# Hyena filter spectra: decay and bias rows spread over the partitions by DMA, and the two filters' last products on the two halves of the array's rows

## The chip, the cores and the metric

The kernel runs on one core of a Trainium2 chip. The time is the device time of one execution in microseconds (us). Three runs of the kernel before gave 2129.68 to 2137.14 us, with a median of 2131.46 us. The engines are named as in the profile: PE multiplies matrices (PEld loads its stationary operand), DVE, ACT and POOL work on tiles, SP issues most of the DMAs.

## The reference

The program is two layers of a hybrid trunk over 256 latent and 256 context tokens of width 1024, in fp32. Each layer modulates the tokens (adaLN), projects them, runs attention, RWKV-7 time mixing and a Hyena long convolution side by side, projects back, and ends with a feed-forward block (dense in layer 0, eight experts in layer 1). The change lies in one small piece, which depends on parameters alone and not on the tokens, the spectra of the Hyena filters:

```
h = sin(hy_freq1 * (z @ hy_w1 + hy_b1))          # z: 256 positions x 33
h = sin(hy_freq2 * (h @ hy_w2 + hy_b2))          # 256 x 64
h = (h @ hy_w3) * exp(-t * hy_decay)             # 256 x 1024: 2 filters x (fwd, bwd) x 256
kern = concatenate([fwd, 0, bwd reversed])       # per filter
kern = kern / sum(abs(kern))
K = rfft(kern)                                   # taken with cosine and sine matrices
y = irfft(rfft(z) * K) + z * hy_bias             # later, in the convolution
```

## The kernel before, in words

An fp32 matmul is one call in the code and two passes in the trace, so a row "x4" of such a matmul is two calls. The weights' products are split into high and low parts and take three matmuls (`mm3`, lines 321 to 323).

A scheduler orders the instructions of each engine ahead of time, from the order in which the program issues them and from priorities; at run time each engine takes its own list strictly in that order and waits by semaphores. Buffers come from rings and pools. Loads on SP are issued behind one another (`behind`).

The program begins with a stage called stage 0 below. It loads 16 pieces of 512 KB of the adaLN weights of layer 0 (`raw`, line 347, "wraw<-in_adaw"). Each piece, once landed, feeds four matmuls of 128 rows by 32 columns ("ada", line 392), and their sums are transposed (`adaT`, line 404) and modulate the context's normalised rows, which start the first projection ("u", line 321). The buffers for the pieces come free when PE has used them. Between the ada matmuls PE works on the first layer's spectra (`spectra`, lines 534 to 612). The second layer's spectra are worked out between the RWKV part of layer 1's context and the end of layer 0's latent feed-forward block, whose last product is "fo".

`spectra` computes, in this order: the first product (p1, line 542, "hf"); the exponential windows exp(-t * decay), for which the decay row lies on one partition and is spread over 128 by two matmuls with a row of ones (line 548, "hf_d"), so that ACT reads the spread row from PSUM in four instructions of 128x512 (line 550); two sines, each reduced on DVE and then taken on ACT (`sin_of`, lines 498 to 513), with the second product between them (line 557); the bias row, spread in the same manner (line 563) and copied by ACT (line 564). Then, in two halves of the positions (tt) and for two filters (od), come the last products with a contraction of 64 (line 575, "hf3"), which DVE multiplies by the windows (line 576). ACT takes absolute values (line 580), POOL adds forward and backward parts (line 581), PE sums them over the positions ("hf_n", line 582), and cosine and sine products follow ("Kc", "Ks", "Kn").

Of the kernel before, what the change touches and what calls it, by code (L numbers as in the profile page):

```python
# [143 lines left out]
def layout(i):  # L144

    g = lambda n: np.asarray(i[n])
    A = {}
    A["cst"] = constants()
    xs = np.stack([g("ctx")[0], g("x")[0]])
    A["xs"] = np.ascontiguousarray(xs.reshape(2, 2, 128, D).transpose(0, 2, 1, 3))  # L150
    cc = np.zeros((128, 8, 32), np.float32)
    cc[:, :, 0] = g("c_ctx").reshape(8, 128).T
    cc[:, :, 1] = g("c")[0].reshape(8, 128).T
    A["cc"] = cc
    aw = g("ada_w").reshape(2, 8, 128, 3, 4, 2, 256)
    A["adaw"] = np.ascontiguousarray(aw.transpose(0, 3, 5, 1, 2, 4, 6))
    ab = np.zeros((2, 3, 128, 512), np.float32)
    b = g("ada_b").reshape(2, 3, 4, 512)
    for j in range(4):
        for s in range(2):  # L160
            ab[:, :, 32 * j + s] = b[:, :, j]
    A["adab"] = ab
    ft = feature_tiles()
    wi = g("w_in")
    wp = np.zeros((2, 1024, 20 * 128), np.float32)
    for n, cols in enumerate(ft):
        m = [q for q, c in enumerate(cols) if c >= 0]
        wp[:, :, [n * 128 + q for q in m]] = wi[:, :, [cols[q] for q in m]]
    A["win"] = np.ascontiguousarray(wp.reshape(2, 8, 128, 20, 128).transpose(0, 3, 2, 1, 4))
    wo = g("w_out")[:, mix_rows()]  # L170
    A["wout"] = np.ascontiguousarray(wo.reshape(2, 4, 2, 128, 2, 512).transpose(0, 4, 1, 3, 2, 5))

    def w13(w1, w3):
        e = w1.shape[0]
        u = np.stack([w1, w3], 1).reshape(e, 2, 4, 2, 128, 11, 256)
        return np.ascontiguousarray(u.transpose(0, 5, 2, 4, 3, 1, 6)).reshape(e, 11, 4, 128, 2, 512)

    def w2(w):
        e = w.shape[0]
        u = w.reshape(e, 11, 2, 128, 2, 512)  # L180
        return np.ascontiguousarray(u.transpose(0, 4, 1, 3, 2, 5))

    A["fw13"] = w13(g("ffn_w1"), g("ffn_w3"))[0]
    A["fw2"] = w2(g("ffn_w2"))[0]
    A["mw13"] = w13(g("moe_w1")[0], g("moe_w3")[0])
    A["mw2"] = w2(g("moe_w2")[0])
    A["rout"] = np.ascontiguousarray(g("moe_router")[0].reshape(8, 128, 8).transpose(1, 0, 2))
    A["rows"] = np.stack([g("ln1_g"), g("ln1_b"), g("ln2_g"), g("ln2_b")], 1)
    pr = np.zeros((2, 128, NPRM), np.float32)

    def pp(name, a, col=0, r0=0):
        pr[:, r0:r0 + a.shape[1], PRM[name] + col] = a

    mu = g("rwkv_mu")
    for m, nm in ((0, "mu0"), (1, "mu1")):
        pp(nm, mu[:, m, 768:864], 0)
        for q, o in enumerate((256, 384, 512, 640)):
            pp(nm, mu[:, m, o:o + 128], 1 + q)
        for q, o in enumerate((0, 128)):
            pp(nm, mu[:, m, o:o + 128], 5 + q)  # L200
    sw, sb = g("hy_short_w"), g("hy_short_b")
    for q, o in enumerate((512, 640, 0, 128, 256, 384)):
        for m in range(3):
            pp(f"hw{m}", sw[:, m, o:o + 128], q)
        pp("hb", sb[:, o:o + 128], q)
    for h in range(2):
        pp("qg", g("q_gain"), 0, 64 * h)
        pp("kg", g("k_gain"), 0, 64 * h)
    for d in range(2):
        for t in range(2):  # L210
            pp("a0", g("rwkv_a0")[:, d, 128 * t:128 * t + 128], 2 * d + t)
    for nm, src in (("kk", g("rwkv_kk")), ("ka", g("rwkv_ka")), ("rk", g("rwkv_rk").reshape(2, 256)),
                    ("gng", g("rwkv_gn_g")), ("gnb", g("rwkv_gn_b"))):
        for t in range(2):
            pp(nm, src[:, 128 * t:128 * t + 128], t)
    pp("b1", g("hy_b1"))
    pp("f1", g("hy_freq1"))
    pp("b2", g("hy_b2"))
    pp("f2", g("hy_freq2"))
    A["prm"] = pr  # L220
    lo = np.zeros((2, 128, 2, 512), np.float32)
    wB, aB, gB = g("rwkv_wB"), g("rwkv_aB"), g("rwkv_gB")
    for d in range(2):
        lo[:, 16 * d:16 * d + 16, 0, 256 * d:256 * d + 256] = wB[:, d]
        lo[:, 32, 0, 256 * d:256 * d + 256] = g("rwkv_w0")[:, d]
        lo[:, 32 + 16 * d:48 + 16 * d, 1, 256 * d:256 * d + 256] = aB[:, d]
    lo[:, 64:96, 1, 0:256] = gB
    A["lora"] = lo
    w12 = np.zeros((2, 64, 128), np.float32)
    w12[:, :33, :64] = g("hy_w1")  # L230
    w12[:, :, 64:] = g("hy_w2")
    A["hy12"] = w12
    A["hy3"] = np.ascontiguousarray(g("hy_w3"))
    A["hydec"] = np.ascontiguousarray(g("hy_decay"))
    A["hyd"] = np.ascontiguousarray(g("hy_bias")).reshape(2, 512)
    return A
# [8 lines left out]
AF = mybir.ActivationFunctionType  # L245
# [250 lines left out]
class Mix(Trunk):  # L496

    def sin_of(s, ps, f, fb, out):

        v = s.nc.vector  # L500
        a = s.k([64, 256], "sn")
        n = s.k([64, 256], "sn")
        v.tensor_scalar(a, ps, f, fb, op0=OP.mult, op1=OP.add)
        M = 12582912.0
        v.tensor_scalar(n, a, 1.0 / (2 * math.pi), M, op0=OP.mult, op1=OP.add)
        v.tensor_scalar(n, n, M, None, op0=OP.subtract)
        hi = float(np.float32(6.28125))
        mid = float(np.float32(2 * math.pi - 6.28125))
        lo = float(2 * math.pi - 6.28125 - mid)
        for cst in (hi, mid, lo):  # L510
            v.scalar_tensor_tensor(a, n, -cst, a, op0=OP.mult, op1=OP.add)
        v.tensor_scalar(a, a, 3.1415925, -3.1415925, op0=OP.min, op1=OP.max)
        s.nc.scalar.activation(out, a, AF.Sin)

    def spec_load(s, l):

        def ld(*a):
            with s.behind():
                s.last = s.nc.sync.dma_start(*a)

        w12 = s.k([64, 256], "sn")
        ld(w12[:, :128], s.A["hy12"][l])
        dr, br = s.k([1, 1024], "hydec"), s.k([1, 512], "hyd")
        ld(dr, s.A["hydec"][l:l + 1])
        ld(br, s.A["hyd"][l:l + 1])

        def rest():
            w3 = s.k([64, 1024], "hy3")
            ld(w3, s.A["hy3"][l])
            return w12, w3, dr, br  # L530

        return rest

    def spectra(s, l, bk, b2, bn, w12, w3, dr, br):

        nc = s.nc
        mm = nc.tensor.matmul
        fb = s.k([128, 2], "hy_fb")
        for i in range(2):
            nc.vector.tensor_mul(fb[:64, i:i + 1], s.pv(l, f"f{i + 1}")[:64], s.pv(l, f"b{i + 1}")[:64])  # L540
        p1 = s.bank(bk, "hf1")[:64, :256]
        mm(p1, w12[:33, :64], s.c("zT")[:33, :], start=True, stop=True)

        wins = [s.k([128, 1024], "hy_w") for _ in range(2)]
        for od in range(2):
            ds = slice(512 * od, 512 * od + 512)
            b = s.bank((b2, bn)[od], "hf_d")
            mm(b, s.c("ones")[0:1, :], dr[:, ds], start=True, stop=True)
            for tt in range(2):
                i = nc.scalar.activation(wins[tt][:, ds], b, AF.Exp, scale=s.c("negt")[:, tt:tt + 1])  # L550
                if s.first is not None:
                    s.order(i, s.first)
                    s.first = None
        h1 = s.k([64, 256], "sn")
        s.sin_of(p1, s.pv(l, "f1")[:64], fb[:64, 0:1], h1)
        p2 = s.bank(bk, "hf2")[:64, :256]
        mm(p2, w12[:64, 64:128], h1, start=True, stop=True)
        h2 = s.k([64, 256], "sn")
        s.sin_of(p2, s.pv(l, "f2")[:64], fb[:64, 1:2], h2)
        rb = s.k([128, 2, 512], "hy_rb")  # L560
        rn, dbc = rb[:, 0], rb[:, 1]
        b = s.bank(b2, "hf_d")
        mm(b, s.c("ones")[0:1, :], br, start=True, stop=True)
        nc.scalar.copy(dbc, b)
        yield

        eo = [s.k([128, 2, 2, 256], "hy_eo") for _ in range(2)]
# [2 lines left out]
        for tt in range(2):  # L570
            hf = s.k([128, 2, 2, 256], "hy_f")
            win = wins[tt]
            for od in range(2):
                p3 = s.bank((bk, b2)[od], "hf3")
                mm(p3, h2[:, 128 * tt:128 * tt + 128], w3[:, 512 * od:512 * od + 512], start=True, stop=True)
                nc.vector.tensor_mul(hf[:, od].rearrange("p d c -> p (d c)"), p3, win[:, 512 * od:512 * od + 512])
                if tt == 0:
                    nc.vector.memset(hf[0:1, od, 1, :], 0.0)
            ab = s.k([128, 2, 2, 256], "hy_ab")
# [10 lines left out]
        for kt in range(2):  # L590
# [7 lines left out]
            p2 = s.bank(b2, "Ks")  # L598
# [1157 lines left out]
```

## Time and profile before

| | |
|---|---|
| median of three runs | 2131.46 us |
| the profiled execution | 2134.47 us |
| its span, first to last instruction | 2132.7 us |
| PE busy | 2033.8 us, 95% of the span |
| DVE, ACT, POOL busy | 1659.7, 1105.6, 111.1 us |
| mean granted TensorE clock | 0.965 of full speed |

The profile is one execution. Its time exceeds its span by 1.8 us and the median by 3.0 us. A granted clock of 1.00 stands for 2.4 GHz and 0.50 for 1.2 GHz. Before the first change of clock the column reads 1.00, whatever the level; there the durations of the matmuls tell it. Matmuls are pipelined, so that a row's duration overlaps the next row by some tenths of a microsecond; the differences of start times give the price.

### The profile page before, as it was taken

What the parts mean: (1) busy time and instruction counts of PE and PEld (TensorE: products, weight loads), DVE (VectorE), ACT (ScalarE), POOL (GpSimd) and SP (SyncE); (2) the same over time, 40 slices, a digit from 0 to 9 for tenths busy, and PEclk for the clock granted to TensorE, in tenths of its full rate; (3) what the DMA queues carried; (4) which work ended last, traced back from release to release, by engine and by line L of the source; (5) the groups of instructions that cost most, each with busy time, mean ns of one, the idle gap of its engine ahead of it and who ended that gap; (6) DMA issues with size and microseconds to landing.
All of it is one profiled execution on the core that took longest, in us unless ns stands there. A gap on an engine that the chain in (4) does not pass through costs nothing. (4 is left out here: it accounts for less than half of the span.)

```text
span 2132.7 us, 35433 instructions
## 1 busy us (share of the span) xinstructions
PE 2033.8 (95%) x13514; PEld 1656.6 (78%) x13514; DVE 1659.7 (78%) x3050; ACT 1105.6 (52%) x1615; POOL 111.1 (5%) x87
## 2 busy tenths in 40 slices
PE   7999999999999999989798997999999999999996
PEld 2878777667878999888487676888888888888885
DVE  6897678469753685776888568799899989988997
ACT  3532445132332434443254232877787877778773
POOL 0012002100000000010101200000000000000000
PEclk9999899899999999999998997999999999999998
DMA  8522332246697545332311038699999999999992
GB/s 302 186 83 90 139 124 83 80 160 230 235 337 269 198 164 200 137 102 94 125 55 38 31 110 316 233 329 356 352 347 367 356 343 347 365 359 339 364 352 103
DMA packets 147850, 469.12 MB, mean 220 GB/s; under 512 B 31636, under 2 KB 33972, under 8 KB 147672
## 3 DMA queue, kind: packets, MB, share of 16 engines
q1 hardware_dynamic: 123512, 446.27, 57.9%
q0 software_dynamic: 4816, 17.36, 2.3%
q10 hardware_dynamic: 19344, 3.15, 0.8%
q8 instruction: 108, 1.77, 0.3%
q14 instruction: 70, 0.57, 0.1%
HBM read 464.56 MB, written 2.16 MB: 219 GB/s over the span
## 5 line engine op out<-in xcount | busy, mean ns | idle before, releaser
L316 DVE TENSOR_TENSOR wlo<-wraw,whi 128x1024 fp32r<-128x1024 f32 x748 | 887.4, 1221 | 83.0 <-ACT whi L315 52.4
L315 ACT CAST whi<-wraw 128x1024 fp32r<-128x1024 f32 x748 | 751.6, 1049 | 146.1 <-DMA wraw<-in_fw_dram 33.8
L321 PE MATMUL ab<-whi,m_x 128*128 128x512 f32 x704 | 281.6, 400 | 0.0
L323 PE MATMUL ab<-whi,m_x 128*128 128x512 f32 x704 | 275.6, 391 | 0.0
L322 PE MATMUL ab<-wlo,m_x 128*128 128x512 f32 x704 | 275.0, 391 | 0.0
L321 PE MATMUL ab<-hp,whi 128*128 128x256 f32 x704 | 204.9, 292 | 3.1 <-ACT hp L315 2.2
L323 PE MATMUL ab<-hp,wlo 128*128 128x256 f32 x704 | 201.8, 288 | 2.8 <-DVE wlo L316 2.8
L322 PE MATMUL ab<-hp,whi 128*128 128x256 f32 x704 | 201.4, 286 | 1.3 <-DVE hp L316 1.2
L321 PE MATMUL u<-hp,whi 128*128 128x256 f32 x512 | 152.0, 300 | 3.9 <-ACT hp L315 3.0
L323 PEld LDWEIGHTS ab<-whi,m_x 128*128 128x128 f32 x704 | 132.2, 188 | 28.3
L322 PEld LDWEIGHTS ab<-wlo,m_x 128*128 128x128 f32 x704 | 132.5, 188 | 25.5 <-DVE wlo L316 0.2
L321 PEld LDWEIGHTS ab<-whi,m_x 128*128 128x128 f32 x704 | 132.2, 188 | 25.1
L321 PEld LDWEIGHTS ab<-hp,whi 128*128 128x128 f32 x704 | 135.7, 193 | 19.0 <-issue 10.6
L323 PE MATMUL u<-hp,wlo 128*128 128x256 f32 x512 | 149.0, 294 | 1.4 <-DVE wlo L316 1.1
L322 PE MATMUL u<-hp,whi 128*128 128x256 f32 x512 | 149.5, 295 | 0.0
L323 PEld LDWEIGHTS ab<-hp,wlo 128*128 128x128 f32 x704 | 136.1, 194 | 6.3 <-DVE wlo L316 3.9
L322 PEld LDWEIGHTS ab<-hp,whi 128*128 128x128 f32 x704 | 136.4, 194 | 2.0 <-DVE hp L316 1.8
L321 PE MATMUL mo<-whi,ffg 128*128 128x512 f32 x352 | 137.8, 391 | 0.0
L323 PE MATMUL mo<-whi,ffg 128*128 128x512 f32 x352 | 137.1, 390 | 0.0
L322 PE MATMUL mo<-wlo,ffg 128*128 128x512 f32 x352 | 137.0, 389 | 0.0
L969 POOL TENSOR_TENSOR rBD<-rAT,cst 128x1024 f32<-128x1024 f32 x28 | 67.2, 2408 | 937.7 <-DVE rTm L959 506.9
L321 PEld LDWEIGHTS u<-hp,whi 128*128 128x128 f32 x512 | 99.6, 196 | 18.2 <-issue 9.6
(396 smaller groups left out, 3536.3 us busy)
## 6 DMA issues: line engine op xcount, KB each, us to landing
wraw<-in_mw_dram SPq DMA_DIRECT2D x495, 512.0 KB, 5.6
wraw<-in_fw_dram SPq DMA_DIRECT2D x132, 512.0 KB, 5.7
wraw<-in_adaw_dram SPq DMA_DIRECT2D x96, 512.0 KB, 4.4
wraw<-in_win_dram SPq DMA_DIRECT2D x64, 512.0 KB, 5.1
wraw<-in_mw_dram POOLq DMA_DIRECT2D x33, 512.0 KB, 6.7
wraw<-in_wout_dram SPq DMA_DIRECT2D x24, 512.0 KB, 4.2
lngb<-in_rows_dram SPq DMA_DIRECT2D x12, 512.0 KB, 7.3
x<-in_xs_dram SPq DMA_DIRECT2D x8, 512.0 KB, 5.6
```

The source lines that it names most:

```text
L315: i = (s.nc.scalar.copy if eng == "a" else s.nc.vector.tensor_copy)(hi, src)
L316: return i, s.nc.vector.tensor_sub(lo, src, hi.bitcast(F32))
L321: mm(out, a[0], b[0], start=start, stop=False, **kw)
L322: mm(out, a[0], b[1], start=False, stop=False, **kw)
L323: mm(out, a[1], b[0], start=False, stop=stop, **kw)
L969: i = nc.gpsimd.tensor_mul(x.rearrange("p u (j t) -> p u j t", j=4), bc(ATu[:, :, m, None, :], [128, 8, 4, 32]), bc(mask.rearrange("p (j t ...
```

## The change

Three things are changed, in both layers. The decay and bias rows are loaded with a DMA that writes the same row into all 128 partitions (128x1024 and 128x512 instead of 1x1024 and 1x512). The three spreading matmuls and the copy of the bias go, and ACT computes a window in one instruction of 128x1024 from SBUF. The second product's weights stand twice side by side (columns 64 to 127 and 128 to 191 of `w12`), so that its result, and the sine of it, lie on both halves of the partitions. The last product's weights are stored with the first filter on partitions 0 to 63 and the second on 64 to 127, and its two matmuls of each half of the positions read rows 0 to 63 and rows 64 to 127 of the array, under the scheduler's high priority.

```diff
--- before.py
+++ after.py
@@ -215,8 +215,9 @@
             pp(nm, src[:, 128 * t:128 * t + 128], t)
     pp("b1", g("hy_b1"))
     pp("f1", g("hy_freq1"))
-    pp("b2", g("hy_b2"))
-    pp("f2", g("hy_freq2"))
+    for h in range(2):
+        pp("b2", g("hy_b2"), 0, 64 * h)
+        pp("f2", g("hy_freq2"), 0, 64 * h)
     A["prm"] = pr
     lo = np.zeros((2, 128, 2, 512), np.float32)
     wB, aB, gB = g("rwkv_wB"), g("rwkv_aB"), g("rwkv_gB")
@@ -226,11 +227,12 @@
         lo[:, 32 + 16 * d:48 + 16 * d, 1, 256 * d:256 * d + 256] = aB[:, d]
     lo[:, 64:96, 1, 0:256] = gB
     A["lora"] = lo
-    w12 = np.zeros((2, 64, 128), np.float32)
+    w12 = np.zeros((2, 64, 192), np.float32)
     w12[:, :33, :64] = g("hy_w1")
-    w12[:, :, 64:] = g("hy_w2")
+    w12[:, :, 64:128] = w12[:, :, 128:] = g("hy_w2")
     A["hy12"] = w12
-    A["hy3"] = np.ascontiguousarray(g("hy_w3"))
+
+    A["hy3"] = np.ascontiguousarray(g("hy_w3").reshape(2, 64, 2, 512).transpose(0, 2, 1, 3)).reshape(2, 128, 512)
     A["hydec"] = np.ascontiguousarray(g("hy_decay"))
     A["hyd"] = np.ascontiguousarray(g("hy_bias")).reshape(2, 512)
     return A
@@ -498,8 +500,9 @@
     def sin_of(s, ps, f, fb, out):
 
         v = s.nc.vector
-        a = s.k([64, 256], "sn")
-        n = s.k([64, 256], "sn")
+        r = out.shape[0]
+        a = s.k([r, 256], "sn")
+        n = s.k([r, 256], "sn")
         v.tensor_scalar(a, ps, f, fb, op0=OP.mult, op1=OP.add)
         M = 12582912.0
         v.tensor_scalar(n, a, 1.0 / (2 * math.pi), M, op0=OP.mult, op1=OP.add)
@@ -519,49 +522,41 @@
                 s.last = s.nc.sync.dma_start(*a)
 
         w12 = s.k([64, 256], "sn")
-        ld(w12[:, :128], s.A["hy12"][l])
-        dr, br = s.k([1, 1024], "hydec"), s.k([1, 512], "hyd")
-        ld(dr, s.A["hydec"][l:l + 1])
-        ld(br, s.A["hyd"][l:l + 1])
+        ld(w12[:, :192], s.A["hy12"][l])
 
         def rest():
-            w3 = s.k([64, 1024], "hy3")
+            w3 = s.k([128, 512], "hy3")
             ld(w3, s.A["hy3"][l])
-            return w12, w3, dr, br
+            dec, bias = s.k([128, 1024], "hydec"), s.k([128, 512], "hyd")
+            ld(dec, s.A["hydec"][l:l + 1].to_broadcast([128, 1024]))
+            ld(bias, s.A["hyd"][l:l + 1].to_broadcast([128, 512]))
+            return w12, w3, dec, bias
 
         return rest
 
-    def spectra(s, l, bk, b2, bn, w12, w3, dr, br):
+    def spectra(s, l, bk, b2, bn, w12, w3, dec, dbc):
 
         nc = s.nc
         mm = nc.tensor.matmul
         fb = s.k([128, 2], "hy_fb")
         for i in range(2):
-            nc.vector.tensor_mul(fb[:64, i:i + 1], s.pv(l, f"f{i + 1}")[:64], s.pv(l, f"b{i + 1}")[:64])
+            nc.vector.tensor_mul(fb[:, i:i + 1], s.pv(l, f"f{i + 1}"), s.pv(l, f"b{i + 1}"))
         p1 = s.bank(bk, "hf1")[:64, :256]
         mm(p1, w12[:33, :64], s.c("zT")[:33, :], start=True, stop=True)
 
         wins = [s.k([128, 1024], "hy_w") for _ in range(2)]
-        for od in range(2):
-            ds = slice(512 * od, 512 * od + 512)
-            b = s.bank((b2, bn)[od], "hf_d")
-            mm(b, s.c("ones")[0:1, :], dr[:, ds], start=True, stop=True)
-            for tt in range(2):
-                i = nc.scalar.activation(wins[tt][:, ds], b, AF.Exp, scale=s.c("negt")[:, tt:tt + 1])
-                if s.first is not None:
-                    s.order(i, s.first)
-                    s.first = None
+        for tt in range(2):
+            i = nc.scalar.activation(wins[tt], dec, AF.Exp, scale=s.c("negt")[:, tt:tt + 1])
+            if s.first is not None:
+                s.order(i, s.first)
+                s.first = None
         h1 = s.k([64, 256], "sn")
         s.sin_of(p1, s.pv(l, "f1")[:64], fb[:64, 0:1], h1)
-        p2 = s.bank(bk, "hf2")[:64, :256]
-        mm(p2, w12[:64, 64:128], h1, start=True, stop=True)
-        h2 = s.k([64, 256], "sn")
-        s.sin_of(p2, s.pv(l, "f2")[:64], fb[:64, 1:2], h2)
-        rb = s.k([128, 2, 512], "hy_rb")
-        rn, dbc = rb[:, 0], rb[:, 1]
-        b = s.bank(b2, "hf_d")
-        mm(b, s.c("ones")[0:1, :], br, start=True, stop=True)
-        nc.scalar.copy(dbc, b)
+        p2 = s.bank(bk, "hf2")[:, :256]
+        mm(p2, w12[:64, 64:192], h1, start=True, stop=True)
+        h2 = s.k([128, 256], "sn")
+        s.sin_of(p2, s.pv(l, "f2"), fb[:, 1:2], h2)
+        rn = s.k([128, 512], "hy_rb")
         yield
 
         eo = [s.k([128, 2, 2, 256], "hy_eo") for _ in range(2)]
@@ -570,10 +565,13 @@
         for tt in range(2):
             hf = s.k([128, 2, 2, 256], "hy_f")
             win = wins[tt]
+            p3 = [s.bank(q, "hf3") for q in (bk, b2)]
+            with s.tc.high_priority():
+                for od in range(2):
+                    r = slice(64 * od, 64 * od + 64)
+                    mm(p3[od], h2[r, 128 * tt:128 * tt + 128], w3[r, :], start=True, stop=True)
             for od in range(2):
-                p3 = s.bank((bk, b2)[od], "hf3")
-                mm(p3, h2[:, 128 * tt:128 * tt + 128], w3[:, 512 * od:512 * od + 512], start=True, stop=True)
-                nc.vector.tensor_mul(hf[:, od].rearrange("p d c -> p (d c)"), p3, win[:, 512 * od:512 * od + 512])
+                nc.vector.tensor_mul(hf[:, od].rearrange("p d c -> p (d c)"), p3[od], win[:, 512 * od:512 * od + 512])
                 if tt == 0:
                     nc.vector.memset(hf[0:1, od, 1, :], 0.0)
             ab = s.k([128, 2, 2, 256], "hy_ab")
```

The scheduler's lists move with it. On SP, at the program's start, the loads of the spectra's parameters (hydec, hyd, and hy for the last product's weights) stand before as follows.

```order
L1584 DMA keep<-in_cc_dram 128x256
L519 DMA sn<-in_hy_dram 64x128
L519 DMA hydec<-in_hydec_dram 1x1024
L519 DMA hyd<-in_hyd_dram 1x512
L1605 DMA cst_68<-in_cst_dram 128x1024
L519 DMA hy_79<-in_hy_dram 64x1024
L1605 DMA keep<-in_cst_dram 128x512
L347 DMA wraw<-in_adaw_dram 128x1024 x3
L1605 DMA cst_67<-in_cst_dram 128x1024
```

They stand now like this:

```order
L1582 DMA keep<-in_cc_dram 128x256
L522 DMA sn<-in_hy_dram 64x192
L1603 DMA cst_68<-in_cst_dram 128x1024
L522 DMA hy_75<-in_hy_dram 128x512
L522 DMA hydec<-in_hydec_dram 128x1024
L522 DMA hyd<-in_hyd_dram 128x512
L1603 DMA keep<-in_cst_dram 128x512
L349 DMA wraw<-in_adaw_dram 128x1024 x3
```

The two rows come after the first constants now, and four entries ahead of the first piece of the adaLN weights (wraw) are as before, but 768 KB large where they were 6 KB.

On PE, in stage 0, the list from the first product to the last products (hf with a number, 128x512, from hy) was this:

```order
L542 MATMUL hf_212<-cst_68,sn 64x256
L548 MATMUL hf_d<-hydec,cst_68 128x512 x2
L563 MATMUL hf_d<-hyd,cst_68 128x512
L392 MATMUL ada<-wraw,keep 32x256 x4
L557 MATMUL hf_232<-sn 64x256
L392 MATMUL ada<-wraw,keep 32x256 x12
L575 MATMUL hf_335<-hy_79,sn 128x512
L575 MATMUL hf_339<-hy_79,sn 128x512
L392 MATMUL ada<-wraw,keep 32x256 x4
L575 MATMUL hf_350<-hy_79,sn 128x512
L392 MATMUL ada<-wraw,keep 32x256 x4
```

It is now this:

```order
L545 MATMUL hf_212<-cst_68,sn 64x256
L394 MATMUL ada<-wraw,keep 32x256
L556 MATMUL hf_226<-sn 128x256
L394 MATMUL ada<-wraw,keep 32x256 x11
L572 MATMUL hf_326<-hy_75,sn 128x512
L572 MATMUL hf_327<-hy_75,sn 128x512
L572 MATMUL hf_341<-hy_75,sn 128x512
L394 MATMUL ada<-wraw,keep 32x256
L572 MATMUL hf_342<-hy_75,sn 128x512
L394 MATMUL ada<-wraw,keep 32x256 x8
L580 MATMUL hf_n<-hy_ab,cst_68 128x512
```

The spreading matmuls are gone. The second product (128x256 now) stands behind one ada matmul instead of four, the last products behind twelve ada matmuls (three pieces) instead of sixteen (four pieces). The first three last products stand together, and the fourth follows one ada matmul later.

On PE, in layer 1, the second half of the last products and what follows up to the sum of the absolute values (hf_n) stood among matmuls of the feed-forward block (fo) like this:

```order
L575 MATMUL hf_9676<-hy_9618,sn 128x512
L323 MATMUL fo<-whi,ffg 128x512
L575 MATMUL hf_9679<-hy_9618,sn 128x512
L321 MATMUL fo<-whi,ffg 128x512
L322 MATMUL fo<-wlo,ffg 128x512
L323 MATMUL fo<-whi,ffg 128x512
L321 MATMUL fo<-whi,ffg 128x512
L322 MATMUL fo<-wlo,ffg 128x512
L323 MATMUL fo<-whi,ffg 128x512
L321 MATMUL fo<-whi,ffg 128x512
L582 MATMUL hf_n<-hy_ab,cst_68 128x512
```

And now, from the fourth last product on:

```order
L572 MATMUL hf_9657<-hy_75,sn 128x512
L325 MATMUL fo<-whi,ffg 128x512
L323 MATMUL fo<-whi,ffg 128x512
L324 MATMUL fo<-wlo,ffg 128x512
L325 MATMUL fo<-whi,ffg 128x512
L323 MATMUL fo<-whi,ffg 128x512
L324 MATMUL fo<-wlo,ffg 128x512
L325 MATMUL fo<-whi,ffg 128x512
L323 MATMUL fo<-whi,ffg 128x512
L324 MATMUL fo<-wlo,ffg 128x512
L325 MATMUL fo<-whi,ffg 128x512
L580 MATMUL hf_n<-hy_ab,cst_68 128x512
```

All four last products are issued with one fo matmul among them, where six stood in the four before, and hf_n follows the fourth after ten fo matmuls instead of seven. The list of PE also differs at many places in the mixing part of layer 0, where the change touches no code.

## Rows read from the trace of the kernel before

**Rows 1.** The page, engines over the span: busy us, share, instructions.

```profile
PE 2033.8 (95%) x13514; PEld 1656.6 (78%) x13514; DVE 1659.7 (78%) x3050; ACT 1105.6 (52%) x1615; POOL 111.1 (5%) x87
```

**Rows 2.** Windows: length; busy of PE, PEld, DVE, ACT, POOL; clock, DMA share, GB/s.

```profile
20.20:30.50 10.30, 10.30 (x39) 2.31 (x38) 6.92 (x14) 2.11 (x2) 2.57 (x2) 0.50 0.90 329
30.50:46.50 16.00, 15.76 (x98) 5.94 (x94) 13.79 (x38) 2.28 (x3) 0.00 (x0) 1.00 0.68 252
...
100.00:480.00 380.00, 365.60 (x3279) 280.70 (x3278) 267.40 (x761) 142.34 (x303) 47.01 (x24) 0.95 0.33 109
...
860.00:1054.50 194.50, 184.76 (x1525) 154.39 (x1523) 144.11 (x299) 81.92 (x137) 20.04 (x10) 0.99 0.34 114
```

**Rows 3.** Timeline of PE in stage 0: start us, duration us, line, operation, wait.

```profile
7.70 3.78 PE L548 MATMUL hf_d<-hydec,cst 1*128 1x512 f32 x4
...
13.11 1.08 PE L392 MATMUL ada<-wraw,keep 128*32 128x256 f32 x8
14.12 1.11 PE L557 MATMUL hf<-sn 64*64 64x256 f32 x2
...
21.78 2.07 PE L575 MATMUL hf<-hy,sn 64*128 64x512 f32 x2
...
37.66 0.64 PE L392 MATMUL ada<-wraw,keep 128*32 128x256 f32 x8
...
46.53 0.66 PE L404 MATMUL adaT<-keep,ada 128*128 128x128 f32 x4 [0.27 <-DVE ada L397]
```

**Rows 4.** Timeline of ACT in stage 0.

```profile
9.80 1.27 ACT L550 ACTIVATE hy_w<-hf_d,cst 128x512 f32<-128x512 f32 x2 [6.42 <-PE hf_d L548]
11.09 1.28 ACT L513 ACT_TABLE_LOAD   x1
...
22.05 1.06 ACT L580 ACTIVATE hy_ab<-hy_f 128x1024 f32<-128x1024 f32 x1 [3.48 <-DVE hy_f L578]
```

**Rows 5.** Window during a load that spreads a 512 KB row block over partitions.

```profile
1017.90:1019.60 1.70, 1.70 (x6) 0.57 (x4) 1.70 (x4) 1.11 (x2) 0.00 (x0) 1.00 1.03 222
```

**Rows 6.** Timeline of PE in layer 1, from the third spreading matmul on.

```profile
1006.32 1.12 PE L548 MATMUL hf_d<-hydec,cst 1*128 1x512 f32 x2
1007.37 0.39 PE L323 MATMUL ab<-hp,wlo 128*128 128x256 f32 x1
...
1015.09 1.98 PE L575 MATMUL hf<-hy,sn 64*128 64x512 f32 x4
1017.00 0.50 PE L321 MATMUL fo<-whi,ffg 128*128 128x512 f32 x1
...
1018.36 1.12 PE L575 MATMUL hf<-hy,sn 64*128 64x512 f32 x2
...
1023.02 1.12 PE L582 MATMUL hf_n<-hy_ab,cst 128*128 128x512 f32 x2 [0.26 <-POOL hy_ab L581]
...
1024.91 1.02 PE L595 MATMUL Kc<-hy_eo,cst 128*128 128x512 f32 x2
1025.77 1.02 PE L600 MATMUL Ks<-hy_eo,cst 128*128 128x512 f32 x2
...
1027.68 1.12 PE L582 MATMUL hf_n<-hy_ab,cst 128*128 128x512 f32 x2 [0.43 <-POOL hy_ab L581]
```

**Rows 7.** Timeline of POOL there, the adds of forward and backward parts.

```profile
1019.63 3.34 POOL L581 TENSOR_TENSOR hy_ab<-hy_ab 128x512 f32<-128x512 f32 x1 [50.68 <-ACT hy_ab L580]
```

**Rows 8.** Timeline of POOL in stage 0, the first of these adds.

```profile
23.19 1.28 POOL L581 TENSOR_TENSOR hy_ab<-hy_ab 128x512 f32<-128x512 f32 x1 [20.69 <-ACT hy_ab L580]
```

**Rows 9.** Timeline of PE at the end of layer 0's latent feed-forward block.

```profile
1053.57 0.39 PE L322 MATMUL fo<-wlo,ffg 128*128 128x512 f32 x1
1053.80 0.39 PE L323 MATMUL fo<-whi,ffg 128*128 128x512 f32 x1
1066.60 0.69 PE L455 MATMUL hT<-keep,xhat 128*128 128x128 f32 x2 [12.41 <-DVE xhat L441]
```

**Rows 10.** Timeline of PE: two products of attention on two row halves.

```profile
1224.85 1.13 PE L774 MATMUL aS<-akv,aq 64*128 64x512 f32 x4
```

## The prediction

> **What bounds the kernel now.** I read the page's engine shares first. PE is busy for 2033.8 of 2132.7 us, and DVE, the next, for 1659.7 [rows 1]. Time is then won or lost on PE, or where PE waits. The windows say where it waits: it has little idle time anywhere, 14.4 of 380 us in the first layer's mixing, 9.7 of 194.5 us in the stretch that holds the second layer's spectra, 0.24 us in the last 16 us of stage 0 [rows 2]. The same windows hold a second limit, the granted clock: it is 0.50 from 20.2 to 30.5 us. Before that the column would read 1.00, but one ada group takes 1.08 us at 13.11 us and 0.64 us at 37.66 us [rows 3], so PE runs at 1.2 GHz from its first matmul until about 30.5 us and at 2.4 GHz behind that. The timelines of stage 0 and of the spectra of layer 1 come last; there each matmul of the change has a price.
>
> **Stage 0, up to the first matmul on adaLN weights.** PE spends 7.70 to 13.11 us on the three spreading matmuls [rows 3], and the first ada group follows at once: PE holds it up, not its load. Without them the load holds it up. Two loads ahead of it grow from 6 to 768 KB. At 366 GB/s (329 at a DMA share of 0.90 from 20.2 us on [rows 2]) that is 2.1 us; at the 222 GB/s that the trace shows while a load spreads rows over partitions [rows 5] it is 3.5 us. How long the first piece has lain there by 13.11 us the rows don't show. The loads up to it are 1.7 MB by their shapes, 4.7 us at 366 GB/s, which from a start at about 5 us is a landing at 9.5 to 11.5 us (an estimate). Then the first ada comes at 11.5 to 13.6 us, and with a landing right ahead of 13.11 us and the slower rate at 16.6 us. I take 11.5 to 13.6 us, no loss, since the three spreading matmuls alone explain why PE was not at the piece before.
>
> ACT has to wait for the decay row in SBUF instead of PSUM. It starts the windows at 9.80 us now [rows 4]. Four instructions of 128x512, two in 1.27 us, become two of 128x1024; an instruction of that size takes 1.06 us at 22.05 us [rows 4], so 2.1 us for 2.5. Two table loads of 1.28 us [rows 4] and the bias copy go as well, since the windows no longer alternate with the sines. If the row lands at 8.8 to 10.1 us, the first sine ends at 8.8 + 2.1 + 1.3 + 0.4 = 12.6 us to 13.9 us, against 12.8 us now; the second product stood at 14.12 us [rows 3] and stands there or up to 1.4 us earlier. The second sine's reduction on DVE hides the remaining table load in the list before as well, so the gain of these edits on the last products is 0.1 to 1.4 us, and I take 0.8.
>
> **Stage 0, from there to its end.** It ends when PE has worked off its list: it has 0.24 us of idle time from 30.5 to 46.5 us [rows 2], so what is taken from the list comes off the end. A last product costs 2.07 us at 1.2 GHz [rows 3]. Two products of attention on two halves of the array's rows take 1.13 us for four passes of 512 columns [rows 10], the price of one product of 512 columns alone, 1.12 us at the same clock [rows 6]; so a pair costs as much as one. In the new list only the first two stand together with nothing between; the fourth is cut off by an ada matmul. That is -2.0 us, with 0 if nothing runs together and -4.1 if both pairs do. In return one more piece (twelve ada matmuls ahead of the last products where sixteen stood) is left for later: +0.6 to +1.1 us [rows 3], I take 0.8. Sum: -0.8 - 2.0 + 0.8 = -2.0 us. Bounds: -1.4 - 4.1 + 0.6 = -4.9, and with no pair and a load 3.5 us late that isn't made up, +3.5 + 1.1, about +5.
>
> Wider operands (the second product to 128 columns, its sine on 128 partitions, two small products of f and b) cost nothing: the duration of an instruction in these rows goes with the free size, 256 as before. If it went with them, the second product would cost its 1.11 us [rows 3] once more.
>
> **Layer 1.** The loads are issued in the feed-forward block, where the DMA is busy for 0.34 of the time [rows 2]; what they cost is hidden, and 3.5 us if not. Three spreading matmuls go. Start to start one costs 1.05 us [rows 6]; three are -3.1 us. The first pair of last products goes from 1.91 us [rows 6] to one product's 1.05: -0.9 us.
>
> One wait grows. hf_n needs POOL's add, and that comes at the end of a chain: last product, DVE's product with the window, ACT's absolute value, POOL. The first last product starts at 1015.09 us [rows 6] and POOL's add runs for 3.34 us from 1019.63 [rows 7], so that hf_n starts at 1023.02, 7.9 us after the first last product, having waited for 0.26 us [rows 6]. With the pair together DVE may have the second filter earlier, by 0.4 us as an estimate from the 0.9 us saved: 7.5 us. PE gets there sooner now: 1.05 for the pair, 2 x 1.05 for the other two, and eleven fo matmuls at 0.23 us start to start [rows 9] make 5.7 us. PE stands for 1.8 us, and the fo matmuls behind hf_n stand with it. For the second hf_n POOL needs another 3.34 us, in which PE has one hf_n, Kc, Ks and one fo, some 0.9 + 1.7 + 0.2 = 2.8 us [rows 6]: 0.5 us more. Both waits are 0.7 us before [rows 6]: net +1.6 us, between 0 (POOL as fast as in stage 0, 1.28 us [rows 8]) and +2.2.
>
> [...]
>
> Layer 1: -3.1 - 0.9 + 1.6 = -2.4 us, between -4.0 and -1.8. It reaches the end: PE is without a gap until the last fo at 1053.80 us, and what follows (12.41 us on DVE up to the next hT [rows 9]) hangs on that matmul.
>
> **The mixing of layer 0.** Its list changes in many places without any change in its work. It has 14.4 us of idle PE [rows 2]; a reshuffle can close or double half of it: 0, between -7 and +7.
>
> **Sum.** -2.0 - 2.4 + 0 = -4.4 us on the profiled 2134.5 us gives 2130.1. That execution is 3.0 us above the median, so against the median, 2127.1 us; I say 2127.
>
> **Rivals.**
> A. The forecast: 2127, own range 2122 to 2132.
> B. Everything pays: both pairs run together in stage 0 and the load is in time (-4.9 for -2.0), hf_n doesn't wait in layer 1 (-4.0 for -2.4), and the new list of the mixing brings -3 of its 7 us. For it: a shorter list on the engine that is busy for 95%. Against it: the fourth product stands apart, and POOL's row. 2131.5 - 4.9 - 4.0 - 3 = 2119.6 us.
> C. The clock rises late. In the rows PE has been at work from 7.70 us on, and without any idle time from 20.2 us, before the clock rises at 30.5 us [rows 2, 3]. The change takes the 5.4 us of spreading matmuls out and puts an idle stretch there. If the clock then doesn't rise until stage 0 is over, the 15.76 us of work from 30.5 to 46.5 us [rows 2] cost what they do at 1.2 GHz. Ada groups go from 0.64 to 1.08 us, a factor of 1.69; products from 1.12 to 2.07 us [rows 3, 6], a factor of 1.85. With 1.75 that is +11.8 us, so 2127.1 + 11.8 = 2138.9 us. It decides the sign if the rise comes more than about 6 us later (each such us costs 0.75 x the work in it). For it: little matmul work until the pieces arrive. Against it: the matmuls from 7.70 to 20.2 us did not raise it either, and the rise may hang on what comes behind 13 us, which stays.
> [...]
> D. The halves don't run together: then the last products cost what they did (+2.0 and +0.9), 2130.0 us. Against it stands the attention's row [rows 10].
>
> **Chances.** A 0.46, B 0.28, C 0.20, D 0.06. What a measurement can tell from no change here is about 0.3%, 6.4 us: 2125.1 to 2137.9. Faster: most of B (0.23) and the low third of A (0.15), 0.38. Slower: C but for its milder end, 0.19. The same: 0.43. The range reaches from the sum of all lower bounds, 2131.5 - 4.9 - 4.0 - 7 = 2115.6, to just past C: 2116 to 2140.
>
> **What would show it.** In the profile after: no hf_d row; ACT with two windows in a row and one table load in stage 0; the first ada between 11.5 and 13.6 us; the first pair at 2.1 us for four passes at 1.2 GHz; adaT, at 46.53 us now [rows 3], near 44.5 us; in layer 1 a wait of hf_n for POOL of about 1.8 us. The hT behind the block at 1066.60 us [rows 9] should come 4 us sooner. It would be wrong if that hT comes later than now, and then the clock of 20 to 47 us or the idle time of 100 to 480 us must show why.

## The result, and the profile after

The change makes the kernel slower. Four runs gave 2150.13 to 2161.56 us, median 2159.09 us, against 2132.14 us before; the ratio is 1.0116, with a 95% interval of 1.008 to 1.0152. That is 25 us more, where 4.4 us less was forecast, and above the range of 2116 to 2140 us. The profiled execution took 2161.56 us, with a span of 2159.8 us.

The page of the kernel after shows hardly any change in work; the busy time of PE is that of [rows 1], and the span is 27 us longer.

```profile
PE 2033.9 (94%) x13502; PEld 1667.3 (77%) x13502; DVE 1663.1 (77%) x3050; ACT 1102.2 (51%) x1607; POOL 106.0 (5%) x87
```

That the busy time is the same hides differences of either sign: less in the first 50 us (32.1 us instead of 40.3), where the spreading matmuls are gone and the clock was higher (1.00 from 20.2 to 30.5 us, 0.50 before [rows 2]), and more in the mixing, as shown next. So PE waits more, or works at another clock. Where it does is found by laying the same instruction of both traces side by side. After stage 0, at 100 us, the trace after is 0.6 us late. At 540 us before, in the dense block of layer 0, it is 30.4 us late, and stays so until 860 us (30.7). Around the spectra of layer 1 it loses 2.6 us more (33.3 at 1060 us) and wins about 6 us back by 1400 us (27.4). The whole loss lies in the mixing of layer 0, in which the change alters no instruction. Windows over that same work, first of the kernel before, then after (columns as in [rows 2]):

```profile
100.00:540.00 440.00, 424.18 (x3631) 328.28 (x3630) 326.12 (x908) 158.06 (x327) 47.01 (x24) 0.96 0.38 127
```

```profile
100.60:570.40 469.80, 437.52 (x3631) 339.66 (x3630) 329.26 (x909) 158.80 (x327) 45.27 (x24) 0.93 0.36 117
```

The counts of instructions agree: it is the same work. PE is idle for 469.8 - 437.5 = 32.3 us instead of 440.0 - 424.2 = 15.8 us, 16.5 us more, and its busy time is 13.3 us longer for the same matmuls, at a granted clock of 0.93 instead of 0.96. In this pair of runs one half of the 30 us is waiting, the other half work at the lower clock. They stand behind one another in the trace after:

```profile
160.00:170.00 10.00, 6.91 (x66) 5.18 (x65) 7.24 (x12) 1.95 (x5) 3.22 (x2) 1.00 0.09 13
170.00:180.00 10.00, 10.00 (x89) 8.47 (x88) 5.46 (x13) 2.24 (x5) 2.34 (x1) 1.00 0.01 2
180.00:190.00 10.00, 8.41 (x53) 7.91 (x54) 5.22 (x27) 3.76 (x10) 3.29 (x2) 0.73 0.00 0
190.00:200.00 10.00, 10.00 (x68) 7.46 (x64) 5.09 (x15) 1.91 (x3) 0.95 (x1) 0.50 0.01 2
200.00:210.00 10.00, 10.00 (x68) 7.71 (x68) 2.60 (x3) 0.37 (x1) 0.00 (x0) 0.58 0.39 136
```

PE is idle for 3.1 us between 160 and 170 us and for 1.6 us between 180 and 190; then the clock is 0.50 for ten microseconds. Before, PE was idle for 0.3 us from 160 to 200 us and its clock stayed at 1.00. But the clock also falls before, a little later, and there PE had no idle time in front of it from 180 us on:

```profile
220.00:240.00 20.00, 20.00 (x129) 15.75 (x127) 10.83 (x27) 6.79 (x15) 0.00 (x0) 0.66 0.02 9
```

So the waits and the lower clock are both seen; that the one brings the other is not shown.

The list of waits of PE names the places, from 100 to 220 us after (who waits, for whom: us in total, times, the longest):

```profile
PE hz L667 <- DVE rTm L1011: 4.2, 1, 4.2
PE rPQ L1029 <- DVE rTT L1018: 1.9, 1, 1.9
PE rN L1069 <- DVE rMx L1064: 1.4, 1, 1.4
```

The longest wait before in that stretch was 1.8 us. The timeline shows what the 4.2 us are, on PE and then on DVE:

```profile
132.44 0.28 PE L325 MATMUL u<-hp,wlo 128*128 128x256 f32 x1
136.89 1.19 PE L667 MATMUL hz<-hY,cst 128*128 128x256 f32 x2 [4.17 <-DVE rTm L1011]
```

```profile
130.40 2.83 DVE L1149 TENSOR_TENSOR rro<-rkf 128x512 f32<-128x512 f32 x1
133.15 0.26 DVE L1012 TENSOR_REDUCE rTm<-rTm 128x8 f32<-128x112 f32 x1
...
135.72 0.42 DVE L648 TENSOR_TENSOR hYt<-Xs,hyK 128x256 f32<-128x256 f32 x1
...
136.33 0.41 DVE L649 TENSOR_TENSOR hY<-hY,hYt 128x256 f32<-128x256 f32 x1
```

The releaser named is rTm, but hz reads hY, which DVE finishes at 136.74 us. The product of Hyena stands on PE at a place in the list where DVE's list has RWKV's steps ahead of hY. Before, the same product ran at 122.80 us and waited 1.7 us. Of the 4.2 us, about 2.1 come from one instruction of DVE: the product rro took 2.83 us while POOL's product rBD ran, and 0.68 us before, when POOL did nothing:

```profile
130.25 2.43 POOL L967 TENSOR_TENSOR rBD<-rAT,cst 128x1024 f32<-128x1024 f32 x1 [4.13 <-PE u L325]
```

```profile
113.41 0.68 DVE L1151 TENSOR_TENSOR rro<-rkf 128x512 f32<-128x512 f32 x1
```

No instruction of the spectra is in these rows (hyK is their result, which DVE only reads); the lists of PE, DVE and POOL fit each other less well.

Where the change is made, the profile after answers to the rows as follows. Stage 0 (compare [rows 3, 4]):

```profile
13.77 1.03 PE L394 MATMUL ada<-wraw,keep 128*32 128x256 f32 x2 [6.54 <-DMA wraw<-in_adaw_dram]
...
19.40 1.98 PE L572 MATMUL hf<-hy,sn 64*128 64x512 f32 x6 [1.33 <-ACT sn L516]
...
45.70 0.66 PE L406 MATMUL adaT<-keep,ada 128*128 128x128 f32 x4 [0.81 <-DVE ada L399]
```

```profile
10.25 2.19 ACT L549 ACTIVATE hy_w<-hydec,cst 128x1024 f32<-128x1024 f32 x2 [7.00 <-DMA hydec<-in_hydec_dram]
12.46 1.28 ACT L516 ACT_TABLE_LOAD   x1
```

The first ada comes at 13.77 us and waits for its load (13.11 before), the windows take 2.19 us and start at 10.25 us, and six passes of last products, three products, take 1.98 us. The clock had risen by 19.4 us in this run, and adaT is 0.83 us earlier than at 46.53. Layer 1 (compare [rows 6 and 7]):

```profile
1052.08 1.98 PE L572 MATMUL hf<-hy,sn 64*128 64x512 f32 x6
...
1058.87 1.12 PE L580 MATMUL hf_n<-hy_ab,cst 128*128 128x512 f32 x2 [0.86 <-POOL hy_ab L579]
```

```profile
1057.54 1.27 POOL L579 TENSOR_TENSOR hy_ab<-hy_ab 128x512 f32<-128x512 f32 x1 [49.28 <-ACT hy_ab L578]
```

Three products for the price of two (1.98 us, as two cost in [rows 6]); hf_n waits 0.86 us for POOL.

### The profile page after: what moved, and what is told of

It reads as the page before. It is cut to its first block, busy times and chain, and to the rows that moved or that the text cites. A ratio compares the mean times of both kernels' runs of the same rounds, so it can differ in the third digit from the quotient of the medians.

```text
span 2159.8 us, 35433 instructions
## 1 busy us (share of the span) xinstructions
PE 2033.9 (94%) x13502; PEld 1667.3 (77%) x13502; DVE 1663.1 (77%) x3050; ACT 1102.2 (51%) x1607; POOL 106.0 (5%) x87
```

## The experiments

**What differs in the lists.** A tile of 257 to 512 elements a partition does not get a buffer of its own. The function k (line 270 before) puts two of them into one of 4 KB and keeps the second half for the next tile of that name:

```
        elif n <= 512:
            m = 4 if n <= 256 else 2
            r = s.packs.setdefault(key, [None, 0])
            if r[1] % m == 0:
                r[0] = s.p.tile([128, m, 1024 // m], dt, name=name, tag=name)
            t = r[0][:, r[1] % m, :]
            r[1] += 1
```

The change makes two tiles that small, w3 (64x1024 to 128x512, name hy3) and rn (half of a 1024 pair to 128x512, name hy_rb). Layer 0's spectra take the first half of each buffer, layer 1's, 1000 us later, the second. The two buffers, 8 KB of each partition, stay taken over the whole of layer 0's mixing, and the scheduler has that much less for the buffers of the mixing. Hence theory M: the held buffers make the scheduler arrange the mixing otherwise, and that costs the time. Its rival S was that the spectra's own changed instructions cost it.

**Each layer with buffers of its own.** The kernel after, with one line changed:

```diff
-        s.fresh("sn", "hyd")
+        s.fresh("sn", "hyd", "hy_rb", "hy3")
```

> The whole change, but layer 1 takes buffers of its own for hy_rb and hy3 instead of the second halves of those that layer 0 took, so that layer 0's two buffers (8 KB of each partition) are given back after stage 0. No instruction differs, and PE's list of the mixing of layer 0 is that of the kernel before again. Theory M (the two held buffers make the scheduler arrange the mixing otherwise, and that costs the time): the 30 us that the trace after loses from 120 to 540 us go, so 2129 to 2136 us. Rival S (the changed instructions of the spectra themselves cost the time, by a late clock or late loads): 2150 to 2162 us, as after.

Measured: ratio to before 0.9981 (0.9956 to 1.0006), median 2132.71 us. The loss is gone, with every instruction of the change in place. The same work in the mixing, window as above:

```profile
103.30:545.00 441.70, 424.54 (x3633) 328.46 (x3633) 326.26 (x909) 157.95 (x327) 45.92 (x24) 0.96 0.38 126
```

Idle time 17.2 us, clock 0.96: as before. Rival S falls.

**The kernel before with 8 KB held.** No instruction of the kernel before is changed, only the buffers:

```diff
-        rb = s.k([128, 2, 512], "hy_rb")
-        rn, dbc = rb[:, 0], rb[:, 1]
+        rn, dbc = s.k([128, 512], "hy_rb"), s.k([128, 512], "hy_db")
```

> The kernel before, with rn and dbc as halves of two buffers that both layers share (hy_rb, hy_db), so that 8 KB of each partition stay taken from stage 0 to layer 1. Every instruction is that of the kernel before; PE's list of the mixing of layer 0 is the one of the kernel after. Theory M: 20 to 35 us slower than before, 2152 to 2167 us. Rival S: 2130 to 2136 us, as before.

Measured: 1.0086 (1.0056 to 1.0117), median 2148.40 us. Slower without any of the change, by 18 us by the ratio, a little below the 20 us named; the median lies below the range as well. In its profiled run the mixing has the same kind of loss, 27.5 us of idle time and a clock of 0.91:

```profile
96.30:567.90 471.60, 444.12 (x3632) 342.73 (x3633) 330.25 (x909) 159.32 (x327) 45.70 (x24) 0.91 0.36 117
```

Its PE has the same longest wait from 96 to 216 us as the kernel after:

```profile
PE hz L668 <- DVE rTm L1012: 3.0, 1, 3.0
```

**The change in one layer at a time.** With one layer changed no half buffer is shared, so theory M foretells no loss from either, and the loss from both together. The edit is a condition on the layer around each changed line (the old code for the other layer), here in part, for layer 0 alone; for layer 1 alone both are (1,):

```diff
+SPREAD, HALVES, PRIO = (0,), (0,), True
...
-            w3 = s.k([128, 512], "hy3")
-            ld(w3, s.A["hy3"][l])
+            if l in HALVES:
+                w3 = s.k([128, 512], "hy3")
+                ld(w3, s.A["hy3"][l])
+            else:
+                w3 = s.k([64, 1024], "hy3")
+                ld(w3, s.A["hy3w"][l])
```

> The change in layer 0 alone; layer 1's spectra as before. No buffer is shared by the layers, and PE's list differs from the one before in stage 0 alone. Theory M: within 2 us of the kernel before (stage 0 of the trace after is 0.5 us behind at 100 us), 2130 to 2135 us. Rival S with its place in stage 0: 2150 us or more.

Measured: 1.0027 (1.0005 to 1.0048), median 2136.07 us.

> The change in layer 1 alone; layer 0's spectra as before. No buffer is shared by the layers, and PE's list of the mixing of layer 0 is as before; that of layer 1 from 860 us on is moved. Theory M: the trace after lost 3 us from 860 to 1060 us and won 5 us back up to 1260 us, so 2126 to 2136 us. Rival S with its place in layer 1: 2150 us or more.

Measured: 0.9979 (0.9954 to 1.0004), median 2128.63 us. Neither comes near 1.0116. Layer 0's part costs about 6 us, a little more than foretold. Layer 1's measures 4.5 us less than before, with an interval from -9.8 to +0.9 us, so that a gain is likely and not shown. In layer 1 alone the two pairs stand by themselves, and show the halves running together:

```profile
1010.31 1.13 PE L606 MATMUL hf<-hy,sn 64*128 64x512 f32 x4
...
1012.72 1.13 PE L606 MATMUL hf<-hy,sn 64*128 64x512 f32 x4
...
1016.76 1.12 PE L619 MATMUL hf_n<-hy_ab,cst 128*128 128x512 f32 x2 [1.10 <-POOL hy_ab L618]
...
1021.42 1.12 PE L619 MATMUL hf_n<-hy_ab,cst 128*128 128x512 f32 x2 [0.26 <-POOL hy_ab L618]
```

Four passes take 1.13 us in each pair, where the first two products took 1.98 us before [rows 6].

**Either part of the change, in both layers; and 4 KB held without any.** Three kernels hold one buffer each, by different tiles, and PE's list of the mixing is the same in all three. The edits: HALVES = (0, 1) without SPREAD; SPREAD = (0, 1) without HALVES; and the kernel before held as above, with "hy_db" added to the names that layer 1 takes afresh.

> The kernel before with rn and dbc in buffers of their own, of which only rn's (hy_rb) is shared by the layers: 4 KB of each partition stay taken from stage 0 to layer 1 instead of 8 KB. Every instruction is that of the kernel before; PE's list of the mixing of layer 0 is a third one. Theory M (what is held costs): between before and the one with 8 KB held, about half of its 18 us if the price goes with the bytes, 2136 to 2146 us. Rival L (a list is a lottery, and the bytes held say nothing of its price): anything from 2125 to 2165 us, the middle no likelier than the ends.

Measured: 1.0128 (1.008 to 1.0177), median 2162.56 us.

> Only the row halves and the doubled second weights, in both layers; the rows of decay and bias are spread by matmuls as before. hy3 is shared by the layers and holds 4 KB; PE's list of the mixing is word for word that of the kernel before with 4 KB held. Theory M: the time of that kernel, less 1 to 2 us for the pairs. Rival S (the spread rows bring the cost): 2128 to 2133 us.

Measured: 1.0123 (1.0077 to 1.0168), median 2158.05 us.

> Only the rows of decay and bias spread by DMA, in both layers; the last products as before. hy_rb is shared by the layers and holds 4 KB; PE's list of the mixing is again that of the kernel before with 4 KB held. Theory M: the time of that kernel within 4 us. Rival S (the spread rows bring the cost): 2150 to 2162 us.

Measured: 1.0139 (1.0095 to 1.0183), median 2165.69 us. Three kernels with different work in the spectra and one list of the mixing have one time, and it is not half of the price of 8 KB, as was expected under theory M, but at least as much.

**12 KB held.** The kernel before with 8 KB held, and the bias row's tile shared as well:

```diff
-        s.fresh("sn", "hyd")
+        s.fresh("sn")
```

> The kernel before with 12 KB of each partition held from stage 0 to layer 1: rn, dbc and the bias row's tile are all halves of buffers that the layers share. Every instruction is as before; the list of the mixing is a fourth one. If the price went with the bytes, more than 4 KB's 27 and 8 KB's 18 us: 2160 us or more. If each list has its own price (rival L): 2140 to 2165 us, in no order with the bytes; a time within 5 us of before would show that a held buffer need not cost anything.

Measured: 1.0171 (1.0134 to 1.0207), median 2165.29 us. 4, 8 and 12 KB cost 1.28, 0.86 and 1.71%. The price isn't in proportion to the bytes: a third of 1.71% is 0.57%, and 4 KB cost at least 0.8%. But the time lies in the range of the price by bytes and 0.3 us above that of rival L, and only the intervals of 8 and 12 KB are clear of each other, so that a price of each list's own, in no order with the bytes, is not shown. All three lists that were measured cost something.

**The list without the held buffers.** The kernel before with its own buffers, and PE's list fixed to that of the kernel with 8 KB held. The edges only order; they add no semaphore. They reach up to layer 1's experts and leave out the spectra's own instructions. DVE, ACT and SP were left to the scheduler. Of the edit, in part:

```diff
+    def pin(s):
+
+        for e, rows in PIN.items():
...
+                    s.tc.add_manual_dep(ts[at], ts[last].name, mybir.DependencyInfo(
+                        mybir.DependencyClass.NoSync, mybir.DependencyReason.DATA), reason="pin")
```

> The kernel before with its own buffers, nothing held from stage 0 to layer 1, but PE's (and POOL's) list fixed by added ordering edges to that of the kernel before with 8 KB held; DVE, ACT and SP are left to the scheduler. Theory M1 (the list by itself costs, through PE's waits in it and the lower clock behind them): as with 8 KB held, 2145 to 2165 us. Theory M2 (the list is harmless, the waits for the fewer buffers cost): 2128 to 2138 us.

Measured: 1.0122 (1.0082 to 1.0163), median 2153.68 us. With nothing held, this list on PE costs at least as much as with 8 KB held. In its profiled run, the fastest of the six, all of the loss in the mixing is idle time, 31.0 us, and the busy time is that of before:

```profile
95.30:551.30 456.00, 425.05 (x3631) 329.14 (x3630) 328.35 (x909) 158.19 (x327) 45.84 (x24) 0.95 0.37 123
```

The largest wait there is another one, since DVE's list is not the same as with the buffers held:

```profile
PE akb L704 <- DVE keep L334: 8.9, 1, 8.9
```

One rival is left here: a list of PE that is fixed while DVE's is not may cost by the misfit alone. The kernel before with its own list fixed in the same way would tell, and was not run; nor was the opposite, the kernel after with PE's list of before.

**Without the loads ahead of the adaLN weights.** Halves in both layers, spread rows in layer 1 alone, buffers of their own:

```diff
+SPREAD, HALVES, PRIO = (1,), (0, 1), True
...
-        s.fresh("sn", "hyd")
+        s.fresh("sn", "hyd", "hy_rb", "hy3")
```

> Halves in both layers, spread rows in layer 1 alone, each layer with buffers of its own: no load is added ahead of the adaLN weights, nothing is held. Theory M: PE's list of the mixing is that of before, stage 0 loses nothing, layer 1 keeps its 3 to 5 us: 2125 to 2131 us. Rival (stage 0 gains by the spread rows): as own_halves or slower, 2130 to 2136 us.

Measured: 0.9976 (0.9941 to 1.0011), median 2131.12 us. It and the kernel with buffers of their own have the same time within their intervals; whether either beats the kernel before is not shown, nor which of the two expectations holds.

**The same work in all twelve profiled runs.** PE's list of the mixing is one of four, and each run has the same work in it (the windows reach from the matmul at 100.0 us before to the one at 540.0 us before):

| PE's list of the mixing | profiled runs | PE idle, us | PE busy, us | granted clock |
|---|---|---|---|---|
| of the kernel before | before, own buffers, layer 0 alone, layer 1 alone, halves in both layers and spread rows in layer 1 | 15.8, 17.2, 15.9, 16.3, 15.2 | 424.2, 424.5, 418.1, 422.4, 410.4 | 0.96, 0.96, 0.97, 0.96, 0.99 |
| with 4 KB held | before with 4 KB held, halves only, spread rows only | 27.0, 30.6, 28.8 | 452.0, 428.5, 443.1 | 0.89, 0.95, 0.91 |
| with 8 KB held | after, before with 8 KB held, the list without the buffers | 32.3, 27.5, 31.0 | 437.5, 444.1, 425.1 | 0.93, 0.91, 0.95 |
| with 12 KB held | before with 12 KB held | 33.4 | 434.3 | 0.93 |

The idle time goes with the list and hardly with the run: 15.2 to 17.2 us with the list of before, 27.0 to 33.4 us with the others, 14 us more in the mean. The busy time, 452.0 us at the lowest clock (0.89) and 410.4 us at the highest (0.99), is 18 us longer in the mean with the other lists, but differs by 14 us among runs of the list of before alone; so the clock's part can't be read from one pair of runs.

## Why the prediction was wrong

**The mixing of layer 0** is the step that failed. It said that the list "changes in many places without any change in its work", that a reshuffle "can close or double half of" 14.4 us of idle time, "0, between -7 and +7". Measured: +30 us in the profiled pair. The row of 14.4 us [rows 2] was right as a measure of what PE's waiting cost in the old list, and no bound on what a new list can add: the other lists wait 27.0 to 33.4 us where that of before waits 15.2 to 17.2. It also left the clock out. In the pair 13 of the 30 us are the same matmuls at a lower granted clock (0.93 for 0.96), and over the twelve profiled runs their busy time is 18 us longer in the mean with the other lists. And the reshuffle wasn't looked into. It was not a side effect without a cause: the diff itself shows w3 and rn going from 1024 to 512 elements, and the function k shows that such tiles share a buffer that lives as long as the later of the two. That this costs, and how much, only the runs show.

**The sum of the local terms** was -4.4 us. With the mixing's list as before, the whole change measured -0.19%, -4.1 us, with an interval from -9.4 to +1.3 us, so that no gain at all is possible too. Since stage 0 lost time where 2.0 us of gain were forecast, the agreement with -4.4 is luck.

**Stage 0, -2.0 us:** the sign is wrong. adaT came 0.83 us earlier than before, but in the run before the granted clock was 0.50 from 20.2 to 30.5 us [rows 2], and in the run after it stayed up (1.00 in the same window). The kernel before with 8 KB held has PE's list of stage 0 of the kernel before, and in its run the clock stayed up as well (1.00). From the first last product to adaT, in that run and in the run after:

```profile
18.08:41.27 23.19, 22.92 (x136) 8.12 (x136) 20.86 (x51) 4.40 (x5) 2.57 (x2) 1.00 0.93 350
```

```profile
19.40:45.70 26.30, 24.01 (x145) 8.17 (x145) 21.24 (x51) 4.40 (x5) 2.56 (x2) 1.00 0.92 327
```

These are 3.1 us more at the same clock, 2.0 of them idle time. It repeats: 26.3 us with layer 0 alone, 23.2 us in the list without the buffers, whose stage 0 is as before. The prediction took it that stage 0 ends when PE has worked off its list, without waits; in the new list PE waits, for POOL before hf_n and for DVE before adaT (0.81 us above, 0.27 us in [rows 3]):

```profile
25.06 1.12 PE L580 MATMUL hf_n<-hy_ab,cst 128*128 128x512 f32 x2 [1.08 <-POOL hy_ab L579]
```

Layer 0 alone is slower by 0.27%. The first ada came at 13.77 us, 0.2 us past the bound of 11.5 to 13.6, but at 12.23 us in the run with buffers of its own and at 12.67 us with layer 0 alone, so that the larger loads alone do not explain the loss. The gain of 0.8 us ahead of the last products isn't seen: they start at 17.86 to 19.43 us in the four profiled runs with spread rows in layer 0, and at 18.07 to 19.76 us in the six with stage 0 as before.

**Layer 1, -2.4 us:** not clear of nothing. Alone it measured -0.21%, about -4.5 us, with an interval that holds 0. In the profile after, the hT behind the block came at 1099.95 us, 33.35 us later than in [rows 9] where 860 us was 30.7 late: 2.7 us lost on the way, though hf_n waited less than forecast; in that of layer 1 alone 1.1 us were won on the same way. hf_n's waits are 0.86 us after and 1.36 us in layer 1 alone, where 2.3 us were forecast, since POOL's first add took 1.27 us, and 2.19 us there, instead of 3.34 us.

**The rivals.** D, the halves don't run together, is refuted by the 1.13 us rows. C, the clock rises late, rests on a wrong reading: the prediction has PE "at 1.2 GHz from its first matmul until about 30.5 us", but in the run before the clock had risen before 20.2 us and fell there, behind a wait of 1.2 us:

```profile
18.62 2.21 PE L575 MATMUL hf<-hy,sn 64*128 64x512 f32 x4 [1.16 <-ACT sn L513]
```

Four passes took 2.21 us, where four took 3.78 us from 7.70 us on [rows 3]. So the clock was up ahead of 20.2 us, and the row at 0.50 shows a fall and not a clock that had yet to rise. What raises or lowers it, no run here shows. The prediction's 1.2 and 2.4 GHz stand for 0.50 and 1.00, as an estimate from start times in the trace before: at 0.50 the u matmuls of 256 columns come every 0.21 us (228.05 to 228.47 us), 1.2 columns a nanosecond; at 1.00 those of 256 come every 0.120 us (123.57 to 124.53 us) and the fo matmuls of 512 every 0.226 us (1052.67 to 1053.80 us), 0.106 us for 256 columns more, 2.4 a nanosecond. A late rise did not make the result either: the clock had risen by 19.4 us in the run after, and near 29 us in the profiled run with buffers of its own, which is as fast as before. What the clock cost, it cost in the mixing, by a way that C does not have. B's three microseconds from the mixing had the wrong sign.

**What stays open:** why each of the three other lists waits longer than that of before; whether their price goes with the bytes held; why the granted clock is lower in them (0.89 to 0.95 against 0.96 to 0.99); and whether PE's list costs by itself or by its misfit with DVE's.

## What to carry to other kernels

When a scheduler makes the order, a change of a tile's size or life is a change to all the work that lives beside it: look for what each new tile shares, and how long the buffer under it is held, before pricing any instruction. A list that moves where the code doesn't is a term of the sum with its own bounds, and the idle time of the old list is not one of them; here three other lists of the same work all waited longer. If the same stretch holds the same work at both ends, compare the idle time and the granted clock there first.

## What was not expected of the hardware

The time of one and the same kernel spreads by more than 1%: 32 runs of the kernel before, beside the first experiments, lay between 2117.23 and 2140.71 us, the lowest with a mean granted clock of 0.972, the highest with 0.961. The clock in stage 0 differs among runs as well: with the same list of PE up to there, it was 0.50 from 20.2 to 30.5 us in the run before and 1.00 in that with 8 KB held, and adaT came at 46.53 and at 41.27 us. In stage 0 the same three products take 3.78 us in one run and 1.98 us in another; here PE's timeline of the kernel with buffers of its own, beside the kernel after (at 19.40 us, above):

```profile
17.86 3.78 PE L572 MATMUL hf<-hy,sn 64*128 64x512 f32 x6 [0.74 <-ACT sn L516]
```

So differences of a few microseconds between two profiled runs mean nothing by themselves, and the experiments above rest on ratios over 6 to 12 runs each.
